# Two-layer hybrid mixer trunk on one core: the head by token tiles, and where the last gate's sums stand

## Chip, core and metric

The kernel runs on one core of one Trainium2 chip, as a single launch. The metric is the device time of an execution in microseconds. The kernel before was run three times: 2843.34, 2848.01 and 2853.46, median 2848.01 us. One further execution was profiled.

## What is computed

A backbone of two layers (D = 2048), for 256 latent tokens x and 256 context tokens ctx. Cut to what matters here:

```python
for li in range(DEPTH):                       # DEPTH = 2
    need_ctx = li < DEPTH - 1                 # layer 1 updates x alone
    shift, scale, gate = split(silu(c) @ w_ada[li] + b_ada[li], 3)
    shift_c, scale_c, gate_c = split(silu(c_ctx) @ w_ada[li] + b_ada[li], 3)
    h = rms_norm(x, g_pre[li]) * (1 + scale) + shift
    hc = rms_norm(xc, g_pre[li]) * (1 + scale_c) + shift_c
    p = h @ w_in[li]
    pc = hc @ w_in[li]                        # layer 1: only the key and value columns
    oa, ob, oh, od = window_attention(p, pc), mla(p, pc), hgrn(p, pc), pooling(p)
    y = merge(p, (oa, ob, oh, od), w_branch[li], w_out[li])
    x = x + gate * rms_norm(y, g_post[li])
    if need_ctx:                              # the same for the context
        xc = xc + gate_c * rms_norm(yc, g_post[li])
```

Everything is float32. In `merge` each branch is multiplied by a SiLU gate, projected to D, weighted by sigmoid gates, summed, and sent through `w_out`.

## The kernel before

All activations are kept transposed, with channels on partitions: 16 channel tiles of 128, and the 512 tokens (256 latent, 256 context) on the free axis. Each large product is made of three matmuls per tile: a weight unit `raw` of 128x2x512 is split into `whi` (on ACT) and `wlo` = raw - whi (on DVE), the activations likewise into `hh` and `hl`, and PE adds hh·whi, hl·whi and hh·wlo. raw, whi and wlo have three buffers each (`wunit`).

**Head.** x and ctx come in 16 loads of 256 KB on SP's queue. For each of four token tiles ACT takes squares, DVE and GpSimd form the reciprocal root, and DVE scales x. Then, for each of 16 channel tiles, PE transposes four blocks (`n0x`), one of each token tile, and one copy of 128x512 takes them to `n0t`, on ACT and DVE in turns. Eight small loads on ACT's queue bring vectors (`SV`, `BV`); PE transposes them (`pv`) and DVE copies them out (`VT`, `BT`).

**Modulation of layer 0.** Scale and shift of a pair of channel tiles are sums over the 2048 rows of `w_ada`: `ada_units` loads four pieces of 512 KB (`adaw`), and PE does 16 matmuls with 256 columns; `ada_turn` transposes the sums (`adaT`) and DVE adds the bias. This is part 1 (scale) and part 0 (shift). Then `start` writes `hh` by ACT and scaled y and `hl` by DVE.

**First projection.** `chunks_by_k` goes through the input columns that are wanted first (12 column tiles in three groups) pair of channel tiles by pair: each pair's products are summed in PSUM (`L0stps`) and added to sums in SBUF, by an ACT copy in the first pair and a DVE addition later. Between the column tiles stand the ada matmuls of the next pair.

**The other modulations.** Scale and shift of layer 1 and the gates of both layers are summed on DVE, in `ada_rest`: an item is a load of 256 KB (`adw`, two buffers) and one multiply-add of 128x512 per row (`adv`; a row for x and one for ctx, for layer 1's gate the one for x). 256 items come in the order gate 0, scale 1, shift 1, gate 1. A set ends with matmuls with ones, DMAs to DRAM and back on GpSimd's queue, a transpose (`adl_2p`) and the biases (`ada_rows`). Items are started by `pump`, at a rate (`PUMP_RATE`) per weight unit, from the middle of layer 0 on; what is left when layer 0's branches are done is pumped there.

**Order.** A scheduler places the instructions of each engine before the run; every engine and every queue goes in order. `urgent` raises priority, `issued_after` holds an instruction back until another has been issued. After the branches of layer 0 (stages m0 to m3 of the merge, `L0m..`) come `project(0, 0)` for x and `project(0, 1)` for the context (`o00p`, `o01p`), then layer 1 and `project(1, 0)`.

## Time and profile before

| what | value |
|---|---|
| median of three runs | 2848.01 us |
| the profiled execution | 2856.63 us |
| its span | 2854.7 us |
| PE, busy | 2800.5 us, 98% |
| DVE, busy | 1684.4 us, 59% |
| ACT, busy | 1082.3 us, 38% |
| POOL (GpSimd), busy | 101.5 us, 4% |
| bytes moved | 457.67 MB, 160 GB/s |

PE is TensorE's matmul side and PEld its weight loads; SP only issues DMAs. PEclk is the clock that TensorE was granted, as a share of the full 2.4 GHz; 0.5 is 1.2 GHz. In a timeline, "xN" puts N like instructions in one row, and an instruction's duration includes its drain, so those of matmuls overlap; their starts tell the pace. The bracket gives the engine's idle time before the row and what ended it.

### The profile page before, as it was taken

The numbers are of one execution on the slowest core, as the hardware profiler recorded it, in microseconds if no ns is written. First come the engines' busy times: TensorE is split into PE (matmuls) and PEld (weight loads), VectorE is DVE, ScalarE is ACT, GpSimd is POOL, SyncE is SP. The second block draws the span as 40 slices with busy tenths as digits, with TensorE's granted clock in tenths as the row PEclk, the third lists the DMA queues.
The fourth block names the chain that finished last, engine by engine and source line by source line (L and its number), as shares of the span: only waits on it lengthen the run. The fifth ranks groups of instructions, "written<-read, shape, count | busy, mean of one in ns | idle before, by whom it ended". The sixth has DMA issues, their size and how long they took to land. (4 is left out here: it accounts for less than half of the span.)

```text
span 2854.7 us, 40340 instructions
## 1 busy us (share of the span) xinstructions
PE 2800.5 (98%) x15693; PEld 2378.7 (83%) x15693; DVE 1684.4 (59%) x2694; ACT 1082.3 (38%) x1660; POOL 101.5 (4%) x188
## 2 busy tenths in 40 slices
...
GB/s 278 311 191 64 80 74 91 75 118 199 154 168 162 162 166 155 180 157 177 174 194 155 156 207 222 140 98 101 89 91 116 198 185 190 182 191 184 196 230 150
DMA packets 309326, 457.67 MB, mean 160 GB/s; under 512 B 22024, under 2 KB 133088, under 8 KB 309136
## 3 DMA queue, kind: packets, MB, share of 16 engines
...
q14 instruction: 67, 0.55, 0.1%
HBM read 443.40 MB, written 11.62 MB: 159 GB/s over the span
## 5 line engine op out<-in xcount | busy, mean ns | idle before, releaser
L450 ACT ACTIVATE whi<-raw 128x1024 fp32r<-128x1024 f32 (+2 forms) x608 | 639.6, 1052 | 1348.5 <-DMA raw<-in_w_in_dram 42.6
L452 DVE TENSOR_TENSOR wlo<-raw,whi 128x1024 fp32r<-128x1024 f32 (+1 forms) x608 | 734.8, 1210 | 655.6 <-ACT whi L450 614.0
L340 DVE SCALAR_TENSOR_TENSOR adv_3a<-adw,csil,adv_3a 128x512 f32<-128x512 f32 x105 | 74.1, 748 | 55.9 <-DMA adw<-in_w_ada_dram 55.6
L340 DVE SCALAR_TENSOR_TENSOR adv_2a<-adw,csil,adv_2a 128x512 f32<-128x512 f32 x105 | 74.3, 748 | 52.9 <-DMA adw<-in_w_ada_dram 52.8
L340 DVE SCALAR_TENSOR_TENSOR adv_1a<-adw,csil,adv_1a 128x512 f32<-128x512 f32 x105 | 74.3, 748 | 49.1 <-DMA adw<-in_w_ada_dram 49.0
L340 DVE SCALAR_TENSOR_TENSOR adv_0a<-adw,csil,adv_0a 128x512 f32<-128x512 f32 x105 | 74.6, 748 | 44.5 <-DMA adw<-in_w_ada_dram 44.2
L465 PE MATMUL L0stps<-hh,whi 128*128 128x512 f32 x192 | 76.2, 404 | 2.2 <-ACT hh L1222 2.2
L466 PE MATMUL L0stps<-hl,whi 128*128 128x512 f32 x192 | 75.4, 396 | 0.5 <-DVE hl L1224 0.4
L468 PE MATMUL L0stps<-hh,wlo 128*128 128x512 f32 x176 | 69.4, 395 | 0.0
L1154 PE MATMUL o01p<-wlo,hh 128*128 128x512 f32 x128 | 50.2, 392 | 2.1 <-DVE wlo L452 2.1
L1154 PE MATMUL o10p<-wlo,hh 128*128 128x512 f32 x128 | 50.0, 391 | 0.5 <-DVE wlo L452 0.5
L1155 PE MATMUL o01p<-whi,hl 128*128 128x512 f32 x128 | 49.9, 390 | 0.0
L1153 PE MATMUL o10p<-whi,hh 128*128 128x512 f32 x128 | 49.8, 389 | 0.0
L1155 PE MATMUL o10p<-whi,hl 128*128 128x512 f32 x128 | 49.8, 389 | 0.0
L1153 PE MATMUL o00p<-whi,hh 128*128 128x512 f32 x128 | 49.8, 389 | 0.0
L1154 PE MATMUL o00p<-wlo,hh 128*128 128x512 f32 x128 | 49.8, 389 | 0.0
L1155 PE MATMUL o00p<-whi,hl 128*128 128x512 f32 x128 | 49.8, 389 | 0.0
L1153 PE MATMUL o01p<-whi,hh 128*128 128x512 f32 x128 | 49.6, 390 | 0.0
L465 PEld LDWEIGHTS L0stps<-hh,whi 128*128 128x128 f32 x192 | 36.5, 191 | 13.2 <-issue 3.3
L466 PEld LDWEIGHTS L0stps<-hl,whi 128*128 128x128 f32 x192 | 36.4, 189 | 9.7 <-DVE hl L1224 2.3
L468 PEld LDWEIGHTS L0stps<-hh,wlo 128*128 128x128 f32 x176 | 33.3, 189 | 8.5 <-issue 1.6
L251 PE MATMUL ada<-adaw,csil 128*32 128x256 f32 x512 | 34.6, 402 | 0.4 <-DMA adaw<-in_w_ada_dram 0.4
...
## 6 DMA issues: line engine op xcount, KB each, us to landing
...
adw<-in_w_ada_dram SPq DMA_DIRECT2D x256, 256.0 KB, 3.5
...
raw<-in_w_in_dram SPq DMA_DIRECT2D x256, 128.0 KB, 2.4
...
```

The costliest lines, as they stand in the source:

```text
L251: last_ada[0] = mm(out=ps[32 * q:32 * q + 32, :256], lhsT=csil32[:, 4 * u + q, :], rhs=raw[:, q, :], start=(u == 0), stop=(u == 3))
L340: stt(out=acc[r], in0=w, scalar=sc, in1=acc[r], op0=ALU.mult, op1=ALU.add)
L450: act(out=hi[:, :, :width], in_=raw[:, :, :width], func=AF.Copy)
L452: tt(out=lo[:, :, :w], in0=raw[:, :, :w], in1=hi[:, :, :w].bitcast(F32), op=ALU.subtract)
L465: mm(out=out, lhsT=w, rhs=xh, start=first, stop=False)
L466: last_main[0] = mm(out=out, lhsT=w, rhs=xl, start=False, stop=last and wd == 64)
L468: last_main[0] = mm(out=out, lhsT=lo[:, kk, o:o + 128], rhs=xh, start=False, stop=last)
L1153: mm(out=pss[t], lhsT=a, rhs=hi[:, kk, :], start=(k == 0), stop=False)
L1154: mm(out=pss[t], lhsT=a, rhs=lo[:, kk, :], start=False, stop=False)
L1155: mm(out=pss[t], lhsT=b, rhs=hi[:, kk, :], start=False, stop=(k == KT - 1))
```

## The change

1. x and ctx come in eight loads of 512 KB into one tile `xin`, which shares its place with `hl`. Squares and scaling are done in pieces of 128x1024. The head goes by token tile: for each, squares, root, scaling, 16 transposes into four PSUM tiles, and 16 copies of 128x128 on ACT and DVE in turns.
2. The eight vector loads are on GpSimd's queue, b_ada first.
3. The first two channel tiles are taken singly: for each, 2 pieces of 512 KB per part with 128 columns, 16 matmuls of 128 columns, and a pass of its own through the column tiles, with sums taken out of PSUM after each pass. The weight units of both passes are the same.
4. `PUMP_RATE` is 1.1. Three of the four sets of `ada_rest` end in layer 0; layer 1's gate goes on at rate 0.4 beside layer 1 with a smaller ring of slots, and each of its column blocks is summed by a matmul as soon as it is complete.

```diff
-PUMP_AT, PUMP_RATE = 7, 1.45
+PUMP_AT, PUMP_RATE = 7, 1.1
...
-    xs = []
-    for half, src in ((0, I["x"]), (1, I["ctx"])):
-        pc = [[slot(f"x0{half}{t}{c}") for c in range(4)] for t in range(2)]
-        with urgent():
+    xin = hp.tile([128, 4, D], F32, name="xin", tag="hl")
+    with urgent():
+        for half, src in ((0, I["x"]), (1, I["ctx"])):
             for t in range(2):
-                for c in range(4):
-                    last_x = nc.sync.dma_start(out=pc[t][c], in_=src[0, 128 * t:128 * t + 128, 512 * c:512 * c + 512])
-        xs.append(pc)
+                for c in range(2):
+                    last_x = nc.sync.dma_start(out=xin[:, 2 * half + t, 1024 * c:1024 * c + 1024], in_=src[0, 128 * t:128 * t + 128, 1024 * c:1024 * c + 1024])
...
-    nc.scalar.dma_start(out=SV[0:32], in_=I["g_pre"].rearrange("l (k p) -> (l k) p", p=128))
-    nc.scalar.dma_start(out=BV[0:96], in_=I["b_ada"].rearrange("l (k p) -> (l k) p", p=128))
-    nc.scalar.dma_start(out=BV[96:128], in_=I["g_post"].rearrange("l (k p) -> (l k) p", p=128))
-    nc.scalar.dma_start(out=SV[32:38], in_=I["mla_q_norm"].rearrange("l (k p) -> (l k) p", p=128))
-    nc.scalar.dma_start(out=SV[38:40], in_=I["mla_kv_norm"])
-    nc.scalar.dma_start(out=SV[40:48], in_=I["hgrn_norm"].rearrange("l (k p) -> (l k) p", p=128))
-    nc.scalar.dma_start(out=SV[48:56], in_=I["pool_scale"].rearrange("l (k p) -> (l k) p", p=128))
-    nc.scalar.dma_start(out=SV[56:72], in_=I["hgrn_lb"].rearrange("l d (k p) -> (l d k) p", p=128))
     VT = const([128, 128], "VT")
     BT = const([128, 128], "BT")
+
+    nc.gpsimd.dma_start(out=BV[0:96], in_=I["b_ada"].rearrange("l (k p) -> (l k) p", p=128))
+    nc.gpsimd.dma_start(out=SV[0:32], in_=I["g_pre"].rearrange("l (k p) -> (l k) p", p=128))
...
+    nc.gpsimd.dma_start(out=SV[56:72], in_=I["hgrn_lb"].rearrange("l d (k p) -> (l d k) p", p=128))
     pv = paux("pv")
...
-    def ada_units(l, part, j, ring):
-
-        c0 = part * D + 256 * j
+    def ada_units(l, part, k0, nk, ring):
+
+        j = k0
+        c0 = part * D + 128 * k0
+        n = 128 * nk
         ps = paux(f"ada{l}_{part}_{j}")
-        for u in range(4):
-            raw = ring(f"adaw{l}_{part}_{j}_{u}", (128, 4, 256))
+        nq = 1024 // n
+        for u in range(KT // nq):
+            raw = ring(f"adaw{l}_{part}_{j}_{u}", (128, nq, n))
             with urgent():
-                nc.sync.dma_start(out=raw, in_=I["w_ada"][l, 512 * u:512 * u + 512, c0:c0 + 256].rearrange("(k p) n -> p k n", p=128))
-            for q in range(4):
-                last_ada[0] = mm(out=ps[32 * q:32 * q + 32, :256], lhsT=csil32[:, 4 * u + q, :], rhs=raw[:, q, :], start=(u == 0), stop=(u == 3))
+                nc.sync.dma_start(out=raw, in_=I["w_ada"][l, 128 * nq * u:128 * nq * (u + 1), c0:c0 + n].rearrange("(k p) n -> p k n", p=128))
+            for k in range(nq * u, nq * u + nq):
+                q = k % 4
+                last_ada[0] = mm(out=ps[32 * q:32 * q + 32, :n], lhsT=csil32[:, k, :], rhs=raw[:, k - nq * u, :], start=(k < 4), stop=(k >= KT - 4))
         S_ = slot(f"adaS{l}_{part}_{j}")
         with urgent():
-            act(out=S_[:, :256], in_=ps[:, :256], func=AF.Copy)
+            act(out=S_[:, :n], in_=ps[:, :n], func=AF.Copy)
         return S_
...
-                if len(sums) == 4:
+                if len(sums) == 4 or len(rs) == 1:
...
+                pumped[0] += 1
+                if pumped[0] == 3:
+                    ring.close()
+                    ring = Ring("s", 3)
...
     def chunks_by_k(w, groups, pre, name):
 
 
-        for _ in pre(0):
+        for _ in pre(0, 1):
             pass
-        for k0 in range(0, KT, 2):
-            nxt = pre(k0 + 2) if k0 + 2 < KT else iter(())
+        turns = [(0, 1), (1, 1)] + [(k, 2) for k in range(2, KT, 2)]
+        for (ka, na), (kb, nb) in zip(turns, turns[1:] + [(0, 0)]):
+            nxt = pre(kb, nb) if nb else iter(())
             pos = 0
+            if ka == 0:
+                units = []
             for gi, (segs, cts, sums) in enumerate(groups):
-                width = max(o + n for o, _, n in segs)
-                hi, lo = wunit([(o, kview(w, k0, c0, n)) for o, c0, n in segs], width)
+                if ka == 1:
+                    hi, lo = units[gi]
+                else:
+                    width = max(o + n for o, _, n in segs)
+                    hi, lo = wunit([(o, kview(w, ka, c0, n)) for o, c0, n in segs], width)
+                    if ka == 0:
+                        units.append((hi, lo))
                 for i, (o, wd, n) in enumerate(cts):
-                    ps = pmain(f"{name}ps{gi}_{i}_{k0}")[:, :n]
-                    for kk in range(2):
-                        k = k0 + kk
-                        prod(ps, hi, lo, kk, o, wd, hk(k, n), lk(k, n), kk == 0, kk == 1)
+                    ps = pmain(f"{name}ps{gi}_{i}_{ka}")[:, :n]
+                    for k in range(ka, ka + na):
+                        prod(ps, hi, lo, k % 2, o, wd, hk(k, n), lk(k, n), k == ka, k == ka + na - 1)
...
+    xt = [slot(f"n0t{k}") for k in range(KT)]
+    for t in range(4):
+        x = xin[:, t, :]
+        ss = small(f"n0ss{t}", 2)
+        for c in range(2):
+            junk = dslot(f"n0j{t}{c}")
+            act(out=junk, in_=x[:, 1024 * c:1024 * c + 1024], func=AF.Square, accum_out=ss[:, c:c + 1])
+            free(junk)
+        tot = small(f"n0tot{t}", 1)
+        nc.vector.reduce_sum(out=tot, in_=ss, axis=AX.X)
+        r = rstd_of(tot, 1, 1.0 / D, f"n0r{t}")
+        for c in range(2):
+            ts(out=x[:, 1024 * c:1024 * c + 1024], in0=x[:, 1024 * c:1024 * c + 1024], scalar1=r, scalar2=None, op0=ALU.mult)
+        for k0 in range(0, KT, 4):
+            ps = pmain(f"n0x{t}_{k0}")
+            for k in range(k0, k0 + 4):
+                nc.tensor.transpose(ps[:, 128 * (k - k0):128 * (k - k0) + 128], x[:, 128 * k:128 * k + 128], ident)
+            for k in range(k0, k0 + 4):
+                o, q = xt[k][:, 128 * t:128 * t + 128], ps[:, 128 * (k - k0):128 * (k - k0) + 128]
+                if k % 2:
+                    act(out=o, in_=q, func=AF.Copy)
+                else:
+                    nc.vector.tensor_copy(out=o, in_=q)
+    hl = hp.tile([128, KT, 512], F32R, name="hl", tag="hl")
...
-    def start(k0):
-        j = k0 // 2
+    def start(k0, nk):
         S_ = []
         for part in (1, 0):
-            with urgent() if j == 0 else contextlib.nullcontext(), issued_after(last_x):
-                S_.append(ada_units(0, part, j, ada_ring))
+            with urgent() if k0 == 0 else contextlib.nullcontext(), issued_after(last_x):
+                S_.append(ada_units(0, part, k0, nk, ada_ring))
             yield
         with urgent():
-            ada_turn(0, j, *S_)
-            for k in (k0, k0 + 1):
+            ada_turn(0, k0, nk, *S_)
+            for k in range(k0, k0 + nk):
...
-    while pump_list:
+    while pumped[0] < 3:
         pump()
     pump_rate[0] = 0.0
...
+    pump_rate[0] = 0.4
     for _ in layer(1, ctx_norm):
         pass
+    while pump_list:
+        pump()
+    pump_rate[0] = 0.0
```

`ada_turn` takes `k0, nk` in the same way as `ada_units`.

**PE at the end of the head.** `n0x` are transposes of x, `ada` and `adaT` the modulation's sums and their transposes, `L0stps` the first projection. Before:

```order
L1198 MATMUL n0x_338<-ident,x_83 128x128
L1198 MATMUL n0x_338<-ident,x_87 128x128
L1198 MATMUL n0x_338<-ident,x_99 128x128
L1198 MATMUL n0x_338<-ident,x_103 128x128
L262 MATMUL adaT_0_409<-ident,adaS_0_0_407 128x128 x2
L465 MATMUL L0stps_0_0_437<-hh,whi_432 128x512
L465 MATMUL L0stps_1_0_472<-hh,whi_432 128x512
L465 MATMUL L0stps_2_0_480<-hh,whi_432 128x512
L465 MATMUL L0stps_3_0_488<-hh,whi_432 128x512
```

Now:

```order
L1221 MATMUL n0x_8_279<-ident,xin 128x128 x4
L265 MATMUL adaT_0_402<-ident,adaS_1_0_377 128x128
L265 MATMUL adaT_0_402<-ident,adaS_0_0_400 128x128
L1221 MATMUL n0x_12_288<-ident,xin 128x128 x4
L1221 MATMUL n0x_0_309<-ident,xin 128x128 x4
L1221 MATMUL n0x_4_318<-ident,xin 128x128 x4
L1221 MATMUL n0x_8_327<-ident,xin 128x128 x4
L1221 MATMUL n0x_12_336<-ident,xin 128x128 x4
L473 MATMUL L0stps_0_0_423<-hh,whi_418 128x512
L474 MATMUL L0stps_0_0_423<-hl,whi_418 128x512
L476 MATMUL L0stps_0_0_423<-hh,wlo_419 128x512
L254 MATMUL ada_1_1_428<-adaw_1_1_0_429,csil_92 32x128 x8
```

The ada matmuls and adaT have moved ahead of the last token tile, so that 16 transposes stand right before the first projection, and the ada matmuls of the next channel tile right behind its first column tile.

**DVE between the first passes.** `L0..<-L0stps` take a column tile's sum out of PSUM; n0t is the y that is scaled for `hl`. Before, between the first and the second pair:

```order
L273 SCALAR_TENSOR_TENSOR aT_157<-adar_1_1_565,VT 128x4
L1223 TENSOR_SCALAR n0t_252<-n0t_252,aT_157,bT_159 128x256 x2
L1224 TENSOR_TENSOR hl<-n0t_252,hh 128x512
L1223 TENSOR_SCALAR n0t_259<-n0t_259,aT_157,bT_159 128x256 x2
L1224 TENSOR_TENSOR hl<-n0t_259,hh 128x512
L452 TENSOR_TENSOR wlo_687<-raw_685,whi_686 128x2x384
L506 TENSOR_TENSOR L0qa_345<-L0stps_0_2_626,L0qa_345 128x512
```

Now, between the pass of channel tile 1 and that of tiles 2 and 3:

```order
L272 TENSOR_TENSOR bT_135<-adar_0_2_658,BT 128x4
L521 TENSOR_TENSOR L0gd_355<-L0stps_2_1_681,L0gd_355 128x512
L521 TENSOR_TENSOR L0gd_355<-L0stps_3_1_686,L0gd_355 128x512
L1245 TENSOR_SCALAR n0t_139<-n0t_139,aT_133,bT_135 128x256 x2
L1245 TENSOR_SCALAR n0t_140<-n0t_140,aT_133,bT_135 128x256
L1246 TENSOR_TENSOR hl<-n0t_139,hh 128x512
L1245 TENSOR_SCALAR n0t_140<-n0t_140,aT_133,bT_135 128x256
L1246 TENSOR_TENSOR hl<-n0t_140,hh 128x512
L460 TENSOR_TENSOR wlo_758<-raw_756,whi_757 128x2x384
L521 TENSOR_TENSOR L0qa_346<-L0stps_0_2_697,L0qa_346 128x512
```

The y and hl of the next two channel tiles, before in front of any addition to the sums, now stand behind the four last additions of the pass.

**DVE in project(0,0).** `wlo` is a weight unit's low part, which PE's o00p needs; `adv` is a sum of layer 1's gate, `o00y` the projection's output. Before:

```order
L452 TENSOR_TENSOR wlo_12823<-raw_12821,whi_12822 128x1024
L452 TENSOR_TENSOR wlo_12841<-raw_12839,whi_12840 128x1024
L1161 TENSOR_TENSOR o00y_12805<-o00p_12659,o00gg_12653 128x512
L1161 TENSOR_TENSOR o00y_12809<-o00p_12660,o00gg_12653 128x512
L452 TENSOR_TENSOR wlo_12859<-raw_12857,whi_12858 128x1024
L452 TENSOR_TENSOR wlo_12877<-raw_12875,whi_12876 128x1024
L452 TENSOR_TENSOR wlo_12895<-raw_12893,whi_12894 128x1024
```

Now:

```order
L460 TENSOR_TENSOR wlo_12684<-raw_12682,whi_12683 128x1024
L343 SCALAR_TENSOR_TENSOR adv_2_0a_12384<-adw_2_0_11_15176,csil,adv_2_0a_12384 128x512
L460 TENSOR_TENSOR wlo_12702<-raw_12700,whi_12701 128x1024
L1176 TENSOR_TENSOR o00y_12666<-o00p_12520,o00gg_12514 128x512
L343 SCALAR_TENSOR_TENSOR adv_2_0a_12384<-adw_2_0_12_15278,csil,adv_2_0a_12384 128x512
L1176 TENSOR_TENSOR o00y_12670<-o00p_12521,o00gg_12514 128x512
L343 SCALAR_TENSOR_TENSOR adv_2_0a_12384<-adw_2_0_13_15347,csil,adv_2_0a_12384 128x512
L460 TENSOR_TENSOR wlo_12720<-raw_12718,whi_12719 128x1024
L343 SCALAR_TENSOR_TENSOR adv_2_0a_12384<-adw_2_0_14_15478,csil,adv_2_0a_12384 128x512
L460 TENSOR_TENSOR wlo_12738<-raw_12736,whi_12737 128x1024
L343 SCALAR_TENSOR_TENSOR adv_2_0a_12384<-adw_2_0_15_15547,csil,adv_2_0a_12384 128x512
L460 TENSOR_TENSOR wlo_12756<-raw_12754,whi_12755 128x1024
```

About one adv now stands ahead of each wlo here; before there were none.

## Rows read from the trace of the kernel before

**Rows 1.** The page's busy times and shares of the span, by engine.

```profile
PE 2800.5 (98%) x15693; PEld 2378.7 (83%) x15693; DVE 1684.4 (59%) x2694; ACT 1082.3 (38%) x1660; POOL 101.5 (4%) x188
```

**Rows 2.** Waits of PE: what for, us in total, times, longest us.

```profile
PE pv L168 <- DMA x<-in_x_dram: 8.8, 1, 8.8
...
PE adl_2p L285 <- DMA adl<-adr: 3.4, 2, 3.0
...
PE L0m1mg3ps L465 <- DVE L0m1sg L1091: 1.9, 1, 1.9
```

**Rows 3.** Windows: start:end, length, busy PE, PEld, DVE, ACT, POOL, PEclk, DMA, GB/s.

```profile
40.00:50.00 10.00, 7.35 (x49) 4.83 (x49) 5.56 (x14) 4.77 (x10) 0.00 (x0) 0.83 0.66 215
50.00:60.00 10.00, 10.00 (x71) 7.37 (x70) 2.91 (x4) 6.33 (x11) 0.00 (x0) 1.00 1.02 339
```

**Rows 4.** PE's timeline, 14 to 86 us: start, duration, operation [idle before <-releaser].

```profile
14.62 0.45 PE L168 MATMUL pv<-ident,SV 128*128 128x128 f32 x1 [8.83 <-DMA x<-in_x_dram]
...
31.26 2.16 PE L1198 MATMUL n0x<-ident,x 128*128 128x128 f32 x9
...
33.92 1.20 PE L1198 MATMUL n0x<-ident,x 128*128 128x128 f32 x9
...
43.18 1.81 PE L465 MATMUL L0stps<-hh,whi 128*128 128x512 f32 x4 [2.20 <-ACT hh L1222]
...
47.72 0.42 PE L251 MATMUL ada<-adaw,csil 128*32 128x256 f32 x4
...
65.46 0.39 PE L465 MATMUL L0stps<-hh,whi 128*128 128x512 f32 x1
...
85.98 0.39 PE L465 MATMUL L0stps<-hh,whi 128*128 128x512 f32 x1
```

**Rows 5.** ACT's timeline and its queue's, the head.

```profile
8.81 0.32 ACTq L164 DMA_DIRECT2D SV<-in_hgrn_lb_dram  x1
...
23.93 0.62 ACT L380 ACTIVATE n01j<-x 128x512 f32<-128x512 f32 x1
```

**Rows 6.** DVE's timeline, the head.

```profile
25.95 1.67 DVE L389 TENSOR_SCALAR x<-x,n01r 128x512 f32<-128x512 f32 x4 [0.66 <-POOL n01r L372]
...
42.67 0.91 DVE L1223 TENSOR_SCALAR n0t<-n0t,aT,bT 128x256 f32<-128x256 f32 x2 [0.67 <-ACT hh L1222]
43.61 0.69 DVE L1224 TENSOR_TENSOR hl<-n0t,hh 128x512 fp32r<-128x512 f32 x1
```

**Rows 7.** DMA issues before 10 and after 85 us: KB, us to landing.

```profile
SV<-in_hgrn_lb_dram ACTq DMA_DIRECT2D x1, 8.0 KB, 5.5
...
cosT<-in_cosT_dram POOLq DMA_DIRECT2D x1, 128.0 KB, 5.6
```

**Rows 8.** GpSimd's timeline at its first DMA issues: start, duration.

```profile
85.75 0.55 POOL L209 DMA_DIRECT2D cosT<-in_cosT_dram  x1
```

**Rows 9.** PE's timeline at layer 1's gate.

```profile
1644.02 0.20 PE L285 MATMUL adl_2p<-ident,adl 16*128 16x16 f32 x1 [2.95 <-DMA adl<-adr]
```

**Rows 10.** Windows behind two of PE's waits, columns as above.

```profile
1060.00:1064.00 4.00, 4.00 (x12) 3.02 (x11) 4.00 (x7) 0.00 (x0) 0.00 (x0) 0.59 0.45 131
1644.00:1648.00 4.00, 3.98 (x11) 2.97 (x12) 2.28 (x5) 0.27 (x1) 0.51 (x1) 0.57 0.97 350
1648.00:1652.00 4.00, 4.00 (x19) 3.28 (x18) 3.51 (x6) 1.16 (x2) 0.08 (x1) 1.00 0.29 107
```

**Rows 11.** DVE's timeline ahead of L0m1mg3.

```profile
1053.97 2.74 DVE L340 SCALAR_TENSOR_TENSOR adv_3a<-adw,csil,adv_3a 128x512 f32<-128x512 f32 x4 [3.63 <-DMA adw<-in_w_ada_dram]
```

**Rows 12.** DVE's timeline, sums with two rows per item (x4 is two items).

```profile
1142.97 2.74 DVE L340 SCALAR_TENSOR_TENSOR adv_0a<-adw,csil,adv_0a 128x512 f32<-128x512 f32 x4 [1.72 <-DMA adw<-in_w_ada_dram]
...
1153.60 2.74 DVE L340 SCALAR_TENSOR_TENSOR adv_0a<-adw,csil,adv_0a 128x512 f32<-128x512 f32 x4 [1.01 <-DMA adw<-in_w_ada_dram]
```

**Rows 13.** Windows in project(0,0) and in layer 1, columns as above.

```profile
1700.00:1800.00 100.00, 97.86 (x446) 80.42 (x445) 67.90 (x91) 53.69 (x83) 14.17 (x24) 1.00 0.65 219
2300.00:2400.00 100.00, 100.00 (x837) 100.00 (x836) 51.51 (x64) 43.57 (x55) 0.00 (x0) 1.00 0.64 187
```

More of the change, by code (lines that the diff above doesn't have):

```diff
@@ L171, in _build @@
     nc.vector.tensor_copy(out=BT, in_=pv[:, 128:256])
+    free(SV_, BV_)
     negh = const([128, 8], "negh")
@@ L175, in _build @@
     nc.gpsimd.memset(ones, 1.0)
-    free(CV_, SV_, BV_, sgc_)
+    free(CV_, sgc_)
     lb = const([128, 8], "lb")
@@ L227, in _build @@
     hh = hp.tile([128, KT, 512], F32R, name="hh")
-    hl = hp.tile([128, KT, 512], F32R, name="hl")
     def kview(w, k, c0, n):
@@ L240, in issued_after, with ada_turn @@
         return tc.issue_after(ins.ins if hasattr(ins, "ins") else ins)
[L242 to L244 removed]
+    def ada_units(l, part, k0, nk, ring):
+        j = k0
+        c0 = part * D + 128 * k0
+        n = 128 * nk
         ps = paux(f"ada{l}_{part}_{j}")
[L246 to L247 removed]
+        nq = 1024 // n
+        for u in range(KT // nq):
+            raw = ring(f"adaw{l}_{part}_{j}_{u}", (128, nq, n))
             with urgent():
[L249 to L251 removed]
+                nc.sync.dma_start(out=raw, in_=I["w_ada"][l, 128 * nq * u:128 * nq * (u + 1), c0:c0 + n].rearrange("(k p) n -> p k n", p=128))
+            for k in range(nq * u, nq * u + nq):
+                q = k % 4
+                last_ada[0] = mm(out=ps[32 * q:32 * q + 32, :n], lhsT=csil32[:, k, :], rhs=raw[:, k - nq * u, :], start=(k < 4), stop=(k >= KT - 4))
         S_ = slot(f"adaS{l}_{part}_{j}")
         with urgent():
[L254 removed]
+            act(out=S_[:, :n], in_=ps[:, :n], func=AF.Copy)
         return S_
[L257 to L259 removed]
+    def ada_turn(l, k0, nk, S1, S0):
+        pt = paux(f"adaT{l}_{k0}")
         for i, S_ in enumerate((S1, S0)):
[L261 removed]
+            for q in range(nk):
                 nc.tensor.transpose(pt[:, 256 * i + 128 * q:256 * i + 128 * q + 128], S_[:, 128 * q:128 * q + 128], ident)
@@ L264, in ada_turn @@
         for i, part in enumerate((1, 0)):
-            red = small(f"adar{l}_{part}_{j}").rearrange("p (a b) -> p a b", b=2)
-            nc.vector.tensor_reduce(out=red, in_=pt[:, 256 * i:256 * i + 256].rearrange("p (c g r) -> p c r g", c=2, g=4)[:, :, 0:2, :], axis=AX.X, op=ALU.add)
-            bias = BT[:, 48 * l + 16 * part + 2 * j:48 * l + 16 * part + 2 * j + 2].unsqueeze(2).to_broadcast([128, 2, 2])
+            red = small(f"adar{l}_{part}_{k0}", 2 * nk).rearrange("p (a b) -> p a b", b=2)
+            nc.vector.tensor_reduce(out=red, in_=pt[:, 256 * i:256 * i + 128 * nk].rearrange("p (c g r) -> p c r g", c=nk, g=4)[:, :, 0:2, :], axis=AX.X, op=ALU.add)
+            bias = BT[:, 48 * l + 16 * part + k0:48 * l + 16 * part + k0 + nk].unsqueeze(2).to_broadcast([128, nk, 2])
             if part == 0:
-                tt(out=bT[l][:, 2 * j:2 * j + 2, :], in0=red, in1=bias, op=ALU.add)
+                tt(out=bT[l][:, k0:k0 + nk, :], in0=red, in1=bias, op=ALU.add)
             else:
                 tt(out=red, in0=red, in1=bias, op=ALU.add)
-                g = VT[:, 16 * l + 2 * j:16 * l + 2 * j + 2].unsqueeze(2).to_broadcast([128, 2, 2])
-                stt(out=aT[l][:, 2 * j:2 * j + 2, :], in0=red, scalar=1.0, in1=g, op0=ALU.add, op1=ALU.mult)
+                g = VT[:, 16 * l + k0:16 * l + k0 + nk].unsqueeze(2).to_broadcast([128, nk, 2])
+                stt(out=aT[l][:, k0:k0 + nk, :], in0=red, scalar=1.0, in1=g, op0=ALU.add, op1=ALU.mult)
     def ada_rows(l, part):
```

27 lines of the change are left out of this document (7 added, 20 removed).

## The prediction, made before the changed kernel was run

> **What bounds the kernel now.** I began with the engines' busy shares: PE is busy 2800.5 of 2854.7 us [rows 1]. No other engine is near that, so the change can win only PE's idle time (about 54 us) and stretches in which PE runs at its lower clock. The waits of PE say what ended the idle time [rows 2]; the windows and PE's timeline say where it lies [rows 3, 4]. Some 33 us of it lie before 50 us: in the head PE waits for the small vectors, then for scaled x, works through transposes mixed with ada matmuls, and starts the first projection (L0stps) only at 43.18 [rows 4]. The other two losses the change touches are adl_2p, 3.4 us in two waits of which one is 2.95 [rows 2, 9], and L0m1mg3, 1.9 us [rows 2]. Such idle time costs twice: in 1644 to 1648 us PE did 11 instructions at a granted clock of 0.57, in the next 4 us 19 at 1.00; in 1060 to 1064 it did 12 at 0.59 [rows 10]. Eight missing matmuls of some 0.21 us are 1.7 us.
>
> **The head, part one: the first projection starts earlier.** Before, the eight vector loads stand on ACT's queue between other work; the last (hgrn_lb) is issued at 8.81 and lands 5.5 us later [rows 5, 7], 14.3, and pv follows at 14.62 [rows 4]. Every transpose stands behind pv on PE, and the first x sums behind pv's copies on DVE. On GpSimd's queue eight issues of 0.55 us [rows 8] from about 1.3 us on end at 5.7; with 5.6 us to landing, as cosT from that queue [rows 7], pv comes at about 11.5, three us sooner.
> Then the token tiles. Before, a transpose group needs all four x tiles, of which the last was scaled at 25.95+1.67=27.6 [rows 6]; 52 of the 64 transposes and 40 ada matmuls came after that, and PE took until 41 for them. After, 48 transposes can be done before the last tile is there, and only 16 follow it. Two bounds. By the last tile: ACT does the same squares, in half the instructions (before, the last one at 23.93 [rows 5]), plus some copies, so the tile is scaled at about 26; 16 transposes at the pace of 9 in 1.20 us [rows 4] are 2.1, the last copy, hh and its wait 1.5, together 29.6. By PE's own backlog: if every gap keeps it at the pace of 9 in 2.16 us [rows 4], then 64 transposes are 15.4, and 32 ada matmuls and the adaT about 5.5; from 14.5, when the first tile may be scaled, that ends at 35.4, and with 1.5 behind it 36.9. I take 32.5, nearer the first bound, since in before the clock did rise between 31 and 34 us, with the transposes dense. That is **10.7 us earlier** (6.3 to 13.6).
>
> **The head, part two: what the single channel tiles give back.** Before, the first pair of channel tiles took from 43.18 to 65.46, 22.3 us, the second from 65.46 to 85.98, 20.5 [rows 4]; (20.5−2x1.93 of ada)/70 is 0.238 us a matmul. The first pair's 22.3 includes 1.7 of lower clock (0.83 in 40 to 50 us [rows 3]). After, channel tile 0 is 35 matmuls (8.3), the ada sums of tile 1 stand inside it (32 instructions, 1.93 by the x32 row [rows 4]; at the low clock twice that), and the clock rises once (1.7). Tile 1 is again 8.3 with two ada sums (3.86). So the pair carries one ada sum more than before: 1.93 (to 3.9). At the boundary behind tile 1, hl of tiles 2 and 3 stands on DVE behind the last sum of tile 1 (the second order shown above): 0.91 for the scaled y, 0.69 for hl [rows 6], twice; some products with hh stand ahead on PE, so 0 to 3, taken 1.6. Twelve more evacuations (8.3 us on DVE at 0.69) come on top of a DVE that was about 40% busy from 40 to 60 us [rows 3]; I put 2 (0 to 4) on tiles 2 and 3 for sums that come late. Sum 1.9+1.6+2=5.5 (1.9 to 10.9). DMA isn't the limit: by tile 2 it has to bring some 14 MB, at the 339 GB/s of 50 to 60 us [rows 3] 41 us, done well before tile 2 is due. **The head nets 10.7−5.5=5 us** (−2 to +10).
> The clock terms rest on those rows alone. The Trainium skill, TensorE: Matmul & The Clock Gate, Part 1, describes the two levels and that the slow one is the default after idleness; the trace agrees (0.57 behind the 2.95 us gap). By it the slow bound, 36.9, would be the one to take if the tile-by-tile head leaves gaps throughout.
>
> **The gate of layer 1.** Before, its chain (sums, to DRAM and back) ends in front of project(0,0): PE reaches adl_2p 52 rows (12 us) behind the sums and waits 2.95 [rows 9], plus 1.7 of clock: 4.6. So the chain takes some 15 us. After, 167 matmuls of 256 columns stand between, by 837 in 100 us [rows 13] 0.12 each: 20 us, more than 15. **4.5 us gained** (3 to 5).
>
> **Layer 0's other sums at 1.1 in place of 1.45.** PE's order from the first rope on is the same, but DVE's sums stand elsewhere. L0m1mg3's wait came from a DVE that had waited 3.63 us for an adw ahead of an evacuation [rows 11]; no sum stands there now: 1.9+1.5 gained. Against it, other places become as dense: **1.5** (−1 to +4).
>
> **What layer 1 and project(0,0) now carry.** 64 adw loads of 256 KB and 64 DVE sums of 0.75. In layer 1 DVE is half idle and DMA at 0.64 [rows 13], so what stands there costs nothing. But some 32 are placed at the end of layer 0 and in project(0,0), about 25 of them within 22 weight units of 12 matmuls (2.72 us): one per 2.4 us, each ahead of a wlo in DVE's order (the third order shown above); behind a sum that waits for its adw, wlo waits, and PE behind it. adw has two buffers. In before, the loop ran two items in some 5.3 us: from the pair at 1142.97 to the pair after next at 1153.60 there are four [rows 12], 2.66 each, with two sums (1.5) each; with one sum of 0.75 it is about 1.95 to 2.3, enough, as long as landing isn't slower than there (175 GB/s) under the 290 to 325 GB/s wanted here. Lead of wlo on PE hides some us. **−3** (0 to −20).
>
> **Sum:** 5+4.5+1.5−3=8. The profiled execution took 2856.63 (span 2854.7), the median of the runs is 2848.01, 8.6 lower; the gain comes off the median: **2840.0**. About 0.3%, 8.5 us, is what a measurement of this kernel can tell from no change, so this is on the edge.
>
> **Rivals.**
> (a) The start's gain is eaten whole: PE stays at 1.2 GHz through the head (36.9), and the two single passes cost 6.3. For it: the gaps of the tile-by-tile head, DVE's order. Head 0: 4.5+1.5−3=3, 2845.
> (b) The start's gain is kept: last-tile bound 13.6, passes 3.5, and project hides its sums (−1): 10+4.5+1.5−1=15, 2833. For it: DVE and ACT are far from full; against it: in-order queues.
> (c) Slower: adw sets the pace of project(0,0). It decides where an item there takes over 2.4+11/25=2.84 us, which eats the other gains of 11; at the pace of 1142 to 1153 plus another half us for the denser DMA, 3.2, the 25 items lose 20: 11−20=−9, 2857. For it: two buffers and the highest density of the program. Against it: one sum instead of two, and wlo's lead.
> (d) The vectors come no earlier from GpSimd, so that the change doesn't do what it says: with twice cosT's landing pv is at 17 and PE's backlog ends at 39.4. Then the head gives 3.8−5.5=−2: 1 in all, 2847. Against it: that queue issued every 0.55 us and cosT still landed in 5.6, so its loads overlap [rows 7, 8]. The Trainium skill, DMA: Bandwidth & Descriptors, section SWDGE vs HWDGE vs iDMA, speaks for it: descriptors that GpSimd's software builds have the slower setup. The trace hardly bears it out: 5.6 against 5.5 for the last from ACT's queue [rows 7]. It would mean a later pv only if the eight shared no time.
>
> **Chances.** My forecast 0.40, (a) 0.24, (b) 0.17, (c) 0.14, (d) 0.05. Faster by over 0.3% (below 2839.5): (b) and half of the forecast less a little for its centre, with a few of (a): 0.41. Within: the rest of the forecast, nearly all of (a) and (d), the milder half of (c): 0.48. Slower (above 2856.5): the worse half of (c) and strays, 0.11. The range for 8 in 10 goes from (b) to the milder (c): 2832 to 2853.
>
> **What the profile after would show.** Right: pv near 11.5, first L0stps at 30 to 34, tile 4 (the third turn) at 79 to 83 instead of 85.98; adl_2p without a wait, in layer 1; L0m1mg3's wait gone; PE over 97% in project(0,0) with DVE's waits for adw under 1 us. Wrong: a first L0stps behind 36 at a granted clock near 0.5, waits of L0stps for hl or DVE's sums of over 3 us, or wlo waits of PE in o00p.

## The result and the profile after

The changed kernel takes 2861.71 us (median of five runs, 2859.53 to 2866.69), the kernel before 2845.19 in the same comparison: ratio 1.0058, 95% interval 1.0039 to 1.0077. It is slower by 16.5 us. The forecast was 2840, the range ended at 2853.

One thing about the traces first. Before's profiled execution took 2856.63 us, and the five runs of this comparison lie between 2843.34 and 2853.46. A second trace of before (run b_again, below) has a span of 2847.3, 7.4 less than the first; 4.3 of these lie ahead of the first rope (the first matmul behind the first projection), the rest in layer 0's merge stages. The first traces of the two kernels therefore differ by only 3.1 us where the timed medians differ by 16.5. Against the second trace the changed kernel's is 10.5 longer. Most of the other 6 is the choice of execution: the changed kernel's profiled one (2859.53) was the fastest of five, the second one of before (2849.29) lay 4.1 above the median. Below, stages are compared with the second trace.

Busy times and waits of PE in the changed kernel (waits: what for, us in total, times, longest), to be held against [rows 1, 2]:

```profile
PE 2804.3 (98%) x15757; PEld 2381.8 (83%) x15757; DVE 1689.8 (59%) x2727; ACT 1082.8 (38%) x1671; POOL 105.4 (4%) x196
```

```profile
PE pcv L142 <- DMA CV<-in_c_ctx_dram: 7.6, 1, 7.6
PE o00p L1169 <- DVE wlo L460: 5.3, 3, 2.3
PE pv L167 <- DMA SV<-in_hgrn_lb_dram: 2.9, 1, 2.9
PE L1ck2tk L642 <- DVE L1ckt L928: 2.7, 1, 2.7
PE n0x L1221 <- ACT n0t L1225: 2.5, 3, 1.9
PE adl_0p L288 <- DMA adl<-adr: 2.4, 1, 2.4
```

pv waits 2.9 us in place of 8.8, adl_2p and L0m1mg3 are gone from the list, as forecast. New is o00p, 5.3 us for wlo, which the prediction had named as a sign that it was wrong; L1ck2tk has grown from 0.7 to 2.7. adl_0p, now the last chain of layer 0, waits 2.4 us where before adl_2p waited about 3. PE's timeline of the head, against [rows 4]:

```profile
10.77 0.44 PE L167 MATMUL pv<-ident,SV 128*128 128x128 f32 x1 [2.91 <-DMA SV<-in_hgrn_lb_dram]
...
13.77 4.10 PE L1221 MATMUL n0x<-ident,xin 128*128 128x128 f32 x18 [2.34 <-DVE xin L1217]
...
24.49 1.47 PE L1221 MATMUL n0x<-ident,xin 128*128 128x128 f32 x12
...
30.65 0.80 PE L473 MATMUL L0stps<-hh,whi 128*128 128x512 f32 x1 [0.61 <-ACT n0t L1225]
...
38.51 1.08 PE L254 MATMUL ada<-adaw,csil 128*32 128x128 f32 x32
...
43.97 0.50 PE L473 MATMUL L0stps<-hh,whi 128*128 128x512 f32 x1
...
57.75 1.20 PE L473 MATMUL L0stps<-hh,whi 128*128 128x512 f32 x4 [0.60 <-ACT hh L1244]
59.51 0.50 PE L474 MATMUL L0stps<-hl,whi 128*128 128x512 f32 x1 [0.56 <-DVE hl L1246]
```

pv comes at 10.77 and the first projection at 30.65, 12.5 us before the 43.18 of [rows 4] and 9.9 before the 40.55 of the second trace. The pass of channel tile 0 runs to 43.97, that of tile 1 to 57.75, and the waits for hh and hl stand there, 0.6 us each.

PE's starts of stages say where the time goes. Each column is a difference of two starts in PE's timeline, in us (L0qa0rp is the first rope, L1m0mg0ps the first merge product of layer 1, L1m2mg0ps one of its last stage):

| kernel | start to L0qa0rp | o00p to o01p: project(0,0) | o01p to L1m0mg0ps: the context's projection, layer 1's branches | L1m0mg0ps to L1m2mg0ps: merge stages | span |
|---|---|---|---|---|---|
| before, second trace | 201.9 | 87.0 | 490.3 | 414.0 | 2847.3 |
| changed | 199.7 | 94.9 | 499.2 | 418.9 | 2857.8 |
| head_only | 199.2 | 87.1 | 490.3 | 414.1 | 2841.1 |
| pump_only | 201.8 | 95.4 | 498.5 | 419.5 | 2863.4 |
| gate_late | 199.3 | 87.0 | 491.3 | 452.3 | 2878.2 |
| late_held | 200.2 | 87.1 | 490.9 | 418.8 | 2843.0 |

The changed kernel enters project(0,0) 10.1 us sooner than the second trace of before (1634.1 against 1644.2), and loses 7.9 there, 8.9 in the next column and 4.9 in the merge stages: 21.7. None of the 8.9 lies in the context's projection; some 7 lie in 60 us of layer 1's branches, from 1985 us on, where 16 of the 64 sums stand. For project(0,0), DVE's waits from 1640 to 1710 us, its timeline over some of them, and the loads there (KB each, median us to landing) show how:

```profile
DVE adv_1a L343 <- DMA adw<-in_w_ada_dram: 17.0, 9, 3.9
DVE adv_0a L343 <- DMA adw<-in_w_ada_dram: 4.8, 5, 1.2
```

```profile
1684.92 0.75 DVE L343 SCALAR_TENSOR_TENSOR adv_1a<-adw,csil,adv_1a 128x512 f32<-128x512 f32 x1 [2.50 <-DMA adw<-in_w_ada_dram]
1685.59 2.35 DVE L460 TENSOR_TENSOR wlo<-raw,whi 128x1024 fp32r<-128x1024 f32 x2
1687.86 1.53 DVE L343 SCALAR_TENSOR_TENSOR adv_1a<-adw,csil,adv_1a 128x512 f32<-128x512 f32 x2
1689.31 1.22 DVE L460 TENSOR_TENSOR wlo<-raw,whi 128x1024 fp32r<-128x1024 f32 x1
1694.39 0.75 DVE L343 SCALAR_TENSOR_TENSOR adv_1a<-adw,csil,adv_1a 128x512 f32<-128x512 f32 x1 [3.87 <-DMA adw<-in_w_ada_dram]
1695.06 1.22 DVE L460 TENSOR_TENSOR wlo<-raw,whi 128x1024 fp32r<-128x1024 f32 x1
```

```profile
raw<-in_w_out_dram SPq DMA_DIRECT2D x22, 512.0 KB, 5.3
adw<-in_w_ada_dram SPq DMA_DIRECT2D x25, 256.0 KB, 4.4
```

A sum waits 3.87 us for its adw, and the wlo behind it, which PE needs, comes after it. In all DVE stood 22 us of these 70 waiting for adw. The landing takes 4.4 us here; in before, from 1129 to 1178 us, the burst of [rows 12], the median was 3.1.

### The profile page after: what moved, and what is told of

The parts are those of the page before. It is cut to its first block, busy times and chain, and to the rows that moved or that the text cites. A ratio compares the mean times of both kernels' runs of the same rounds, so it can differ in the third digit from the quotient of the medians.

```text
span 2857.8 us, 40467 instructions
## 1 busy us (share of the span) xinstructions
PE 2804.3 (98%) x15757; PEld 2381.8 (83%) x15757; DVE 1689.8 (59%) x2727; ACT 1082.8 (38%) x1671; POOL 105.4 (4%) x196
## 4 chain that ended last, share of the span: by engine, by line
PE 84%; issue 8%; DMA 3%; DVE 3%; POOL 1%; ACT 1%; SPq 0%; DVEq 0%; POOLq 0%; ACTq 0%
PE L0stps L473 1%; PE L0stps L474 1%; DMA adw<-in_w_ada_dram 1%; PE L0stps L476 1%; PE ada L254 1%; PE o10p L1170 1%; PE o10p L1168 1%; PE o10p L1169 1%; PE o01p L1169 1%; PE o01p L1170 1%; PE o01p L1168 1%; DMA raw<-in_w_in_dram 1%; DVE wlo L460 1%; PE L0m1mg1ps L473 1%; PE L0m3mg2ps L473 1%
## 5 line engine op out<-in xcount | busy, mean ns | idle before, releaser
L1169 PEld LDWEIGHTS o00p<-wlo,hh 128*128 128x128 f32 x128 | 24.4, 191 | 11.7 <-DVE wlo L460 6.6
```

The costliest lines, as they stand in the source:

```text
L1169: mm(out=pss[t], lhsT=a, rhs=lo[:, kk, :], start=False, stop=False)
```

## Experiments

The times are medians. The kernel before was timed beside each run (2847.8 to 2850.2), and ratios and their 95% intervals are against that.

**b_again**: the kernel before once more, no edit.

> The kernel before, profiled once more. Its profiled execution took 2856.6 us, but the median of five runs is 2845.2, so the trace of before may hold some 11 us that a usual execution doesn't have. If so, this profile's span is about 2845 and shows a place that is 11 us shorter than in the first trace (one stretch, or the head). If the profiled executions of before are always long, the span is again about 2855.

Span 2847.3. The first trace was long by 7.4 us; the lengths of its stages from o00p on are the same to 0.1 us.

**head_only** and **pump_only** split the change in two. head_only:

```diff
-PUMP_AT, PUMP_RATE = 7, 1.1
+PUMP_AT, PUMP_RATE = 7, 1.45
...
-                if len(sums) == 4 or len(rs) == 1:
+                if len(sums) == 4:
...
-    while pumped[0] < 3:
+    while pump_list:
...
-    pump_rate[0] = 0.4
...
```

pump_only makes the opposite edits in the kernel before.

> The changed head (token tiles, vectors on GpSimd's queue, single first channel tiles) with before's pump: rate 1.45 and all four sets in layer 0. By the two traces the head gains 6.5 us at the first rope; theory 1 (what is lost lies in the sums of layer 1's gate, in project(0,0) and at the start of layer 1) expects 2845-6.5, so about 2839, 0.3% faster. Theory 2 (the head itself costs time that the first trace of before hid) expects 2850 to 2862.

> Before's head with the changed pump: rate 1.1, three sets in layer 0, layer 1's gate at rate 0.4 beside layer 1. Theory 1 expects the whole loss and the head's gain missing: 2861.7+6.5, about 2868, 0.8% slower. Theory 2 expects 2840 to 2846: gate's chain 4.5 and L0m1mg3's 3.5 gained, some of it lost in project(0,0).

head_only: 2841.4 (11 runs) against 2847.8, ratio 0.9977 (0.9968 to 0.9986), 6.5 us faster. pump_only: 2870.5, ratio 1.0080 (1.0067 to 1.0094), 22.7 slower. -6.5 and +22.7 add up to +16.2, against +16.5 for the change; the intervals (some 2.6, 4 and 5 us either way) are wider than that agreement. Theory 1 holds: the head doesn't lose, and the loss is in the sums' new place. Not all of the 6.5 is the head's own, though. At the first rope head_only's trace is 2.7 us ahead of the second trace of before; 3.0 more come in layer 0's merge stages, where the wait of L0m1mg3 (1.7 in the second trace) is gone, although the pump is as before.

**gate_late**: the sums of layer 1's gate kept out of project(0,0) and of layer 1's branches. Each load stands behind last_raw, the last load of a weight unit issued when the item is pumped; 57 of the 64 sums end up in the merge stages.

```diff
-                with urgent():
+                with urgent(), (issued_after(last_raw[0]) if pumped[0] == 3 else contextlib.nullcontext()):
...
+    second = layer(1, ctx_norm)
+    for _ in range(PUMP_AT):
+        next(second)
     pump_rate[0] = 0.4
-    for _ in layer(1, ctx_norm):
+    for _ in second:
```

> The changed kernel, with the loads of layer 1's gate queued behind the weight loads of layer 1's merge stages, so that no sum of it stands in project(0,0) or in layer 1's branches. In the trace of after these two places lose 7.9 and about 8 us against before, and a further 4.7 at the start of the merge stages. Theory 1 expects 2861.7-16 to -20, about 2843, level with before or faster. Theory 2 expects no more than 3 us of change, 2859.

2880.4, ratio 1.0113 (1.0099 to 1.0127): 18.7 us slower than the change instead of 16 to 20 faster. As the table shows, project(0,0) and the branches are as in before, and the merge stages take 38 us more. So theory 1 had named the places, not the cause: there DVE is about half idle [rows 13], and still a sum costs more than anywhere else (38 us for 57; 7.9 for 25 in the changed kernel's project(0,0)). Its waits of DVE from 2200 to 2660 us, 160 us for adw in all:

```profile
DVE adv_1a L344 <- DMA adw<-in_w_ada_dram: 48.1, 12, 5.5
...
DVE adv_3a L344 <- DMA adw<-in_w_ada_dram: 42.8, 13, 5.0
DVE adv_2a L344 <- DMA adw<-in_w_ada_dram: 33.1, 13, 5.3
DVE adv_0a L344 <- DMA adw<-in_w_ada_dram: 27.1, 8, 4.8
```

**gate_noload** and **gate_8col** tell DVE's waiting from its work.

```diff
+                if (l, part) == (1, 2):
+                    loads[i] = prev_w[0]
+                    return
```

```diff
+                elif len(rs) == 1:
+                    stt(out=acc[r][:, :8], in0=w[:, :8], scalar=sc, in1=acc[r][:, :8], op0=ALU.mult, op1=ALU.add)
```

> The changed kernel without the 64 loads of layer 1's gate: its sums read the tile that the set before loaded last, so their DVE work (64 x 0.75 us) stays, at much the same places, and nothing waits for adw. Theory L (what costs is that DVE, in order, waits for adw in front of a wlo or of a sum out of PSUM) expects the loss back: 2861.7-17 to -22, about 2842, as head_only. Theory V (the 0.75 us of DVE work itself where DVE is busy) expects 2857 or more. This leaves out part of the computation: layer 1's gate is formed from other rows.

> The changed kernel with all loads of layer 1's gate, but the sums add only 8 of 512 columns (about 0.15 us in place of 0.75): DVE still waits for each adw at the same place. Theory L expects little change, 2857 to 2862. Theory V expects 2845. This leaves out most columns of layer 1's gate.

2845.7 (10 runs) and 2862.1: theory L, in the main. Work taken away (a sum took 0.22 us in place of 0.75) brings nothing in all; loads taken away bring 16 us. Two limits. gate_8col needs 90.0 us for project(0,0) against 94.9, but loses 3.1 just ahead of it and 3.1 in the merge stages, so its stages don't say what the work costs where. And gate_noload keeps 6.9 of the 21.7: nothing in project(0,0), 4.1 in the branches (L1ck2tk waits 2.8 there, 2.7 in the changed kernel) and 2.8 in the merge stages. In the branches, where DVE waited only 3.3 us for adw, about half of the loss is thus not the wait for loads; the sums' own work and their place in DVE's order are what is left, and no run tells these two apart. gate_noload takes the loads' traffic away with the waits; late_held, below, tells these two apart.

**head_pairs** and **head_act** undo one part of the head each, in head_only.

```diff
-        turns = [(0, 1), (1, 1)] + [(k, 2) for k in range(2, KT, 2)]
+        turns = [(k, 2) for k in range(0, KT, 2)]
```

```diff
-    nc.gpsimd.dma_start(out=BV[0:96], in_=I["b_ada"].rearrange("l (k p) -> (l k) p", p=128))
+    nc.scalar.dma_start(out=BV[0:96], in_=I["b_ada"].rearrange("l (k p) -> (l k) p", p=128))
...
```

> head_only with the first two channel tiles as a pair (4 pieces of 512 KB per part with 256 columns), all else as in head_only: token tiles and vectors on GpSimd's queue stay. In head_only the first projection starts 12.5 us earlier than in the first trace of before, and 6 of that are gone by the first rope. If the two single passes are what gives it back, the pair starts later (its ada sums are twice as long) but runs denser: 2839 to 2842, equal. If the single passes are what wins, 2845 to 2848.

> head_only with the eight vector loads on ACT's queue again, b_ada still first. By the prediction's step, pv comes at 14.3 in place of 10.8, and everything behind it by up to 3 us later: 2843.5. If ACT's order puts the loads ahead of the squares and pv isn't what the first token tile waits for, 2841, no change.

head_pairs: 2839.7 (2839.3 to 2840.7), ratio 0.9968 (0.9957 to 0.9980), the lowest median of all. Its first projection starts at 32.77, 2.1 later than with single tiles, and its first rope at 196.2, 3.0 sooner. The timed intervals overlap, but the traces are clear: with pairs the first rope comes at 195.7 to 196.5 (three traces), with single tiles and this head at 198.8 to 200.4 (ten). So the single tiles cost more than they give; the token tiles and the vectors' move carry the gain. head_act: 2842.6 (2840.2 to 2846.6): the vectors' move is worth about 1 us, and its interval (0.9969 to 0.9987) overlaps head_only's. In its trace pv comes at 14.60 and the first rope at 203.2, 4.0 later than in head_only, but the spans are equal (2841.2 and 2841.1).

**gate_pool** and **late_pool** take the loads off SP's queue, in the changed kernel and in gate_late.

```diff
-                    nc.sync.dma_start(out=w, ...)
+                    (nc.gpsimd if (l, part) == (1, 2) else nc.sync).dma_start(out=w, ...)
```

> The changed kernel with the 64 loads of layer 1's gate issued from GpSimd's queue in place of SP's. In the trace of after, from 1640 to 1710 us, SP's issues of raw wait 18.7 us for wlo, and adw's stand behind them; DVE's sums wait 22 us for adw and hold up the next wlo: a loop over DVE, SP and DMA. Theory S (this loop through SP's queue makes adw late) expects most of the loss back, 2846 to 2851. Theory B (two buffers and the time to landing alone) expects 2860 or more, since a load from GpSimd lands no sooner.

> gate_late with those loads on GpSimd's queue, each behind a GpSimd copy that reads the weight unit's whi, so that the sums stand at the same places in layer 1's merge stages. In gate_late SP's raw issues wait 238 us for wlo between 2250 and 2650. Theory S expects 2842 to 2855 in place of 2880; theory B expects 2872 or more.

2878.3 and 2906.4, slower by 16.6 and 26. Theory S falls. In gate_pool GpSimd issues each load 0.3 us behind the end of the sum before last, which frees its buffer; the loads land in 3.3 us, sooner than SP's 4.4 and not "no sooner", and DVE still waits 22 us in project(0,0). Why it is slower than with SP's queue, not equal, I didn't settle; in late_pool each load also stands behind a copy that waits for whi.

**late_3buf** and **gate_3buf**: a third buffer, and two loads ahead.

```diff
+                if wring[0] and i % 3 == 2:
+                    w = wring[0](f"adw{l}_{part}_{j}_{k}")
+                else:
+                    w = wp.tile([128, 512], F32, name=f"adw{l}_{part}_{j}_{k}", tag="adw", bufs=2)
...
-            load(i + 1)
+            for i2 in range(i + 1, i + (3 if wring[0] else 2)):
```

> gate_late (2880.4) with a third buffer for the gate's adw tiles and two loads ahead of the sum in place of one, the loads on SP's queue and the sums at the same places in layer 1's merge stages. The loads from GpSimd's queue didn't help: there each issue follows the sum that frees its buffer within 1 to 2 us, and DVE still waits for its landing. Theory B (one load ahead is too little for a landing of 4.5 us) expects DVE's waits for adw, 124 us between 2250 and 2650 in gate_late, to fall below 40, and 2845 to 2860. Theory D (DMA itself is full there, so that any load in layer 1 costs) expects 2870 to 2880.

> The changed kernel with the same third buffer; with one slot less for the sums the scheduler puts some 18 in project(0,0) and the rest in layer 1. Theory B expects 2845 to 2853 in place of 2861.7; theory D 2858 to 2862.

gate_3buf: 2851.3 (10 runs), 10.5 less than the change and inside theory B's range. Only 10 sums stand in its project(0,0), but there the buffer also helps: a sum stands 8.9 us behind its load's issue (median) in place of 4.7, and waits 0.6 us on average in place of 0.9. late_3buf: 2871.7, inside theory D's range. Its waits from 2200 to 2660 us:

```profile
DVE adv_3a L350 <- DMA adw<-in_w_ada_dram: 40.2, 14, 4.7
DVE adv_1a L350 <- DMA adw<-in_w_ada_dram: 35.0, 11, 4.7
DVE adv_0a L350 <- DMA adw<-in_w_ada_dram: 27.1, 7, 5.8
DVE adv_2a L350 <- DMA adw<-in_w_ada_dram: 26.9, 11, 4.7
```

129 us in place of the 151 that the same four groups have in gate_late: with a buffer more, DVE waits nearly as long, so theory B fails here. The reason stands in the order. SP's queue and DVE's in gate_late, the same stretch (adw_2_1_5 is the load, adv with it its sum):

```text
SP:  L458 DMA raw_18996 / raw_19026 / adw_2_1_4 / raw_19059 / raw_19089 / adw_2_1_5 / raw_19122
DVE: adv(adw_2_1_4) / wlo(raw_18996) / wlo(raw_19026) / adv(adw_2_1_5) / wlo(raw_19059) / wlo(raw_19089)
```

raw has three buffers, so raw_19089 is issued when wlo(raw_18996) is done, and adw_2_1_5 behind it. On DVE its sum stands behind wlo(raw_19026), one weight unit later: 2.9 us at the pace of before (24 matmuls of 0.12) for a load of 4.7. The same place in the timelines of SP's queue and of DVE:

```profile
2314.50 0.37 SPq L458 DMA_DIRECT2D raw<-in_w_in_dram  x1
2314.92 0.46 SPq L327 DMA_DIRECT2D adw<-in_w_ada_dram  x1
```

```profile
2313.26 2.35 DVE L461 TENSOR_TENSOR wlo<-raw,whi 128x1024 fp32r<-128x1024 f32 x2
2319.20 0.75 DVE L344 SCALAR_TENSOR_TENSOR adv_1a<-adw,csil,adv_1a 128x512 f32<-128x512 f32 x1 [3.59 <-DMA adw<-in_w_ada_dram]
```

The load is issued at 2314.92, DVE has done the second wlo at 2315.61, and the sum starts at 2319.20. With the third buffer a sum in the merge stages still has one wlo between its load's issue and itself, and stands 5.3 us behind the issue (median; 5.2 in gate_late): the load and the sum moved forward together. That the scheduler places a sum where it reckons the load to have landed is my reading of this; no run shows what it reckons.

**late_held** holds the sum, too: gate_late with two buffers and

```diff
+            with issued_after(last_lo[0]) if pumped[0] == 3 else contextlib.nullcontext():
                 for r in rs:
```

where last_lo is the wlo of the unit during which the item is pumped. **late_held_pairs** is the same with the pair of first channel tiles.

> gate_late (2880.4) with two buffers as before, and each sum of layer 1's gate held on DVE behind the wlo of the weight unit during which it is pumped. In gate_late SP issues a load behind the raw of weight unit n, which waits for the wlo of unit n-3, and DVE has the sum of it in front of the wlo of unit n-1: one unit (2.9 us) between issue and use, against a landing of 4.7. Here the sum stands behind the wlo of unit n+2, five units (14 us) later. Theory P (it is the place of the sum against its own load that costs) expects DVE's waits for adw to be under 10 us in all and 2838 to 2846. Theory D (any load beside layer 1 costs) expects 2868 or more.

> late_held with the first two channel tiles as a pair. head_pairs was 1.7 us faster than head_only, so theory P expects 2836 to 2844, and perhaps the fastest of all: the merge stages of layer 0 carry a quarter less, the chain in front of project(0,0) is gone. Theory D expects 2866 or more.

2847.6 (11 runs), ratio 0.9994 (0.9985 to 1.0003), 1.6 us above theory P's range, but 32.7 us less than gate_late, from one place of an instruction. A sum now stands 13.6 us behind its load's issue (median), with five wlo between, and none waits for adw. DVE's timeline in gate_late and then in late_held:

```profile
2565.78 0.75 DVE L344 SCALAR_TENSOR_TENSOR adv_3a<-adw,csil,adv_3a 128x512 f32<-128x512 f32 x1 [3.87 <-DMA adw<-in_w_ada_dram]
2566.45 3.67 DVE L461 TENSOR_TENSOR wlo<-raw,whi 128x1024 fp32r<-128x1024 f32 x3
2575.09 0.75 DVE L344 SCALAR_TENSOR_TENSOR adv_3a<-adw,csil,adv_3a 128x512 f32<-128x512 f32 x1 [4.97 <-DMA adw<-in_w_ada_dram]
2575.76 0.75 DVE L1107 TENSOR_TENSOR L1m3sg<-L1m3yb1ps,L1m3sg 128x256 f32<-128x256 f32 x2
```

```profile
2565.20 1.23 DVE L462 TENSOR_TENSOR wlo<-raw,whi 128x1024 fp32r<-128x1024 f32 x1 [1.65 <-ACT whi L460]
2566.34 0.75 DVE L345 SCALAR_TENSOR_TENSOR adv_3a<-adw,csil,adv_3a 128x512 f32<-128x512 f32 x1
2568.08 1.23 DVE L462 TENSOR_TENSOR wlo<-raw,whi 128x1024 fp32r<-128x1024 f32 x1 [0.99 <-ACT whi L460]
2570.96 1.23 DVE L462 TENSOR_TENSOR wlo<-raw,whi 128x1024 fp32r<-128x1024 f32 x1 [1.66 <-ACT whi L460]
2572.11 0.75 DVE L345 SCALAR_TENSOR_TENSOR adv_3a<-adw,csil,adv_3a 128x512 f32<-128x512 f32 x1
2573.84 1.23 DVE L462 TENSOR_TENSOR wlo<-raw,whi 128x1024 fp32r<-128x1024 f32 x1 [0.99 <-ACT whi L460]
```

In the first, two waits of 3.87 and 4.97 us stand in front of wlo and of L1m3sg, which empties a PSUM bank. In the second no sum waits, and the idle time stands in front of wlo, for whi. The same windows, 2250 to 2650 us, gate_late and late_held:

```profile
2250.00:2650.00 400.00, 379.08 (x3038) 369.53 (x3037) 217.50 (x278) 155.09 (x189) 1.52 (x3) 0.99 0.65 205
```

```profile
2250.00:2650.00 400.00, 400.00 (x3307) 395.85 (x3306) 239.20 (x304) 170.90 (x211) 3.06 (x6) 1.00 0.73 217
```

PE is full again while DMA carries more (217 GB/s against 205): theory D falls, with the same loads in the same stages. The sums aren't free: the merge stages take 418.8 us against 414.1 in head_only, and late_held is 6 us above head_only. late_held_pairs: 2844.0, ratio 0.9978 (0.9970 to 0.9987), again below late_held and not below head_pairs.

**best**: head_pairs with the chain in front of project(0,0) covered.

```diff
-PUMP_AT, PUMP_RATE = 7, 1.45
+PUMP_AT, PUMP_RATE = 7, 1.6
...
         yield
         yield
+        yield
+        yield
         pt = paux(nm + "p", 2)
```

> head_pairs with all four sets in layer 0 at rate 1.6, and two more steps of the pump between the read-back from DRAM and adl_2p: PE then reaches adl_2p 73 matmuls (16.6 us) behind the sums, more than the 15 us of the chain. It takes away the wait for adl_2p (2.1 in head_only, 3 in before) and the lower clock behind it (1.7): 2839.7-4, about 2836. If the denser sums cost as much in the merge stages of layer 0, 2840.

2841.3 (2839.4 to 2846.3), ratio 0.9974 (0.9964 to 0.9985). No adl is left among PE's waits, but project(0,0) starts at 1635.9, against 1633.7 in head_pairs: denser sums in layer 0 take back what the chain gave. head_pairs keeps the lowest median; the intervals overlap.

## Point by point

- **The start of the first projection: right.** pv at 10.77 (forecast 11.5), first L0stps at 30.65 (32.5; bounds 29.6 and 36.9). The transposes at 24.49 run at the faster pace, 12 in 1.47 us, so PE kept up with the tiles, and the last tile's bound was the one that counted. One reading was wrong without consequence: of PE's idle time 22.7 us lie before 50 us (it was busy 27.3 there), not 33.
- **What the single tiles give back: the right size against the first trace, too small against the second.** From tile 0 to tile 2 it took 27.1 us where before's pair took 22.3 [rows 4], 21.0 in the second trace. The third turn starts at 79.32, inside the 79 to 83 named, against 85.98 in the first trace and 82.05 in the second. So 5.9 or 7.2 us of the start's gain are given back by then (forecast 5.5), and 6.7 or 2.7 are left (forecast 5). Timed alone, the head brings 6.5 (forecast 5, -2 to +10), but 3 of it by the trace in layer 0's merge stages, which the head's sum didn't hold: as a number for the head it is partly luck.
- **The gate's chain and layer 0's other sums: right in sum, by luck in the parts.** pump_only reaches o00p at 1637.4, the second trace of before at 1644.2: 6.8 us, forecast 4.5+1.5. But 5.1 of it are gained in layer 0's merge stages before 1605 us (forecast 1.5; the two traces of before differ by 3.0 there). The gate's chain nets 1.6 (forecast 4.5): 5.1 are gained where adl_2p waited, and 3.5 lost where adl_0p now waits 3.0. L0m1mg3's wait is gone as forecast, but in head_only as well, without the lower rate.
- **What layer 1 and project(0,0) carry: the step that failed.** It stood at -3 (0 to -20) and is about -21.7 by the trace, -29.5 by the timed runs (22.7 of pump_only and the 6.8 gained ahead). Three things in it were wrong. It said that in layer 1 DVE is half idle and DMA at 0.64, "so what stands there costs nothing"; but some 14 of the 21.7 us were lost in layer 1, and in gate_late 38 in its emptiest stretch. Idle time of an in-order engine isn't room for an instruction that waits: what counts is the time between a load's issue and its use in the order. In the branches the sums cost 4.1 us even with no load to wait for (gate_noload). Second, for project(0,0) it reckoned 1.95 to 2.3 us a sum with two buffers, if loads landed as fast as in layer 0. The 25 sums there came 2.8 us apart, with 4.4 us to landing in place of 3.1: the two buffers were a limit there, as it had said (SP's issues of adw waited 31 of the 70 us), and the pace was mis-sized. In the merge stages, where it reckoned nothing, late_3buf shows that a third buffer changes little while the sum moves up with its load. Third, "lead of wlo on PE hides some us": a wlo behind a waiting sum also holds back the loads behind it. In gate_late a raw is issued at 2314.50, as the wlo that stood behind the sum ends, and the next adw behind it. How much of the loss that adds isn't shown: SP's raw loads wait for wlo 238 us from 2250 to 2650 in gate_late, but 226 in late_held, too, where it costs nothing.
- **Rival (c)** named the mechanism, sums that wait ahead of wlo, at 0.14 and 2857, with project(0,0) alone as its place. Its mark, 2.84 us an item there, was nearly met (2.8), and the stage lost 7.9 (11 by that mark); the rest came in layer 1. It should have been asked of each place where the sums stand. **(a), (b), (d)** are out by head_only: the start's gain was neither lost nor kept whole, and the vectors came earlier. The rule behind (d), slower setup of GpSimd's descriptors (the Trainium skill, DMA: Bandwidth & Descriptors, SWDGE vs HWDGE vs iDMA), decided nothing here: gate_pool's loads from GpSimd landed in 3.3 us from issue, those of the change from SP in 4.4.
- **The base.** The sum was made against one profiled execution and its gain taken off the median, which the second trace bears out for the stages from project(0,0) on. pump_only's two differences (16.1 in the traces, 22.7 timed) lie 6.6 us apart mostly because the execution profiled (2865.34) was the fastest of its five, 5.2 below their median; where in it those 5.2 us lie, no trace shows.
